# A hybrid encoder layer in one kernel: the helper sum T2 of the last product is stored one step later and made in other steps, and pieces of w_down are loaded and split two per step

## The chip, the core and the metric

The kernel runs on one core of a Trainium2 chip. A time is the device time of one execution in microseconds (us), lower is better. It is taken as the median of several executions.

## What is computed

The reference is one encoder layer on 2048 tokens of width 1024. Two attention mixers run side by side, one with grouped queries and one differential, and a channel mixer follows. The change lies in the last line, the product with w_down (4096 x 1024).

```python
mixed = jnp.concatenate([out_a, out_b], axis=-1)
x = x + jnp.einsum('bse,ed->bsd', mixed, w_out[l])
h = rmsnorm(x, mlp_norm_g[l])
u = jnp.einsum('bsd,df->bsf', h, w_up[l])
u = jnp.square(jax.nn.relu(u))
x = x + jnp.einsum('bsf,fd->bsd', u, w_down[l])
```

## The kernel before

Every large product is done in fp32 by three passes over two parts of each operand: a high part (a cast by ACT, L155) and a low part (the difference, by DVE, L156). `split` makes such a pair, `in_place` does it for a tile that was loaded into its own low half.

The last product, `mlp_down`, multiplies the stored u by w_down with Strassen's scheme in Winograd's form: seven products in place of eight, in the order B11, B21, B22, T2, T3, T1, T4 (`ORDER`). This text numbers them 0 to 6 by i. The right-hand operand of a product is a block of w_down or a sum of blocks (`TERMS`): B11, B21 and B22 are single blocks, T3, T1 and T4 are differences of two terms, and T2 = B22 - (B12 - B11) has three. T2 is needed twice, as the operand of product 3 and as the second term of T4, so it is made once, stored to the scratch tensor wt_d and read back under the name "00". Each operand is cut into 16 **pieces** of 128 x 512, numbered k.

Each product has 8 **steps**, one for each block of 128 tokens (b = 0 to 7), so there are 56 steps, numbered m = 8i + b. A step is 48 matmuls of PE (L1151): 16 pieces times three passes. All 16 pieces of product i are used in each of its 8 steps. The pieces of product i+1 are loaded and split during the steps of product i.

The order on each engine is that of the written code (`manual_schedule`). The main players in the loop of `mlp_down` are:

- SP issues every DMA (L58), in order. A DMA that must wait for its buffer, or a store that must wait for its data, holds up everything written behind it on SP.
- `u_load(m + 2)` loads the u operand of step m+2 (1 MB). The pool has three such buffers, so that load waits until PE has finished step m-1. `u_split(m + 1)` splits the operand of the next step on ACT and DVE.
- `t2(k)` loads three blocks (one tile wd_a, two tiles wd_b), makes two subtractions on POOL (L1124, L1125) and returns the store to wt_d as a function to be called later.
- `prepare_piece(i + 1, k)` loads a piece into a tile wd_a, and for a two-term operand also a tile wd_b, which POOL subtracts (L1016).
- `fill_piece(i + 1, k)` splits a prepared piece into its place as operand (tiles w_op or wd_q).
- `x1` loads a block of the residual for the products that produce output, and `finish` adds the result (L1082) or copies it (L1103); its stores to out are issued after the matmuls of the next step.

The pool of wd_a has seven buffers and that of wd_b two; both go round, and a load waits until its buffer's last reader is done.

In the kernel before, `t2(m)` runs in each of the first 16 steps, and its store is issued at the end of the same step (the list `behind`). Pieces 0 to 5 are loaded one per step in steps b = 0 to 5, pieces 8, 9 and 10 in step 5 too, pieces 6, 7, 11 and 12 in step 6, and 13 to 15 in step 7. Pieces 0 to 5 are split one per step in steps 1 to 6, the other ten in step 7.

Of the kernel before, what the change touches and what calls it, by code (L numbers as in the profile page):

```python
# [48 lines left out]
class Builder:  # L49
# [1013 lines left out]
    def mlp_down(self):  # L1063
        nc, ap = self.nc, self.ap
        H = 512
        NK = DFF // 256
        out = ap["out"]
        with ExitStack() as es:
            pool = self.pools(es)
            self.da, self.db, keep, xp = pool("dra", 7), pool("drb", 2), pool("dk", 1), pool("dx", 4)  # L1070
            psd = pool("psd", 4, space=PSUM)
            es.enter_context(self.tc.manual_schedule())
            U = [keep.tile([P, H], F32, name=f"U{b}") for b in range(8)]
            y12 = [keep.tile([P, H], F32, name=f"y12_{b}") for b in range(8)]

            def rows(half, b):

                t0 = (b // 4) * 1024 + half * 512 + (b % 4) * P
                return slice(t0, t0 + P)

            def plus(t, a, b, e=nc.vector):
                e.tensor_tensor(t, a, b, ALU.add)  # L1082


            goes = {"B21": (0, 0), "B22": (0, 1), "T1": (1, 1), "T4": (1, 0)}

            def x1(i, b):
                n = self.ORDER[i]
                if n not in goes:
                    return None  # L1090
                half, dh = goes[n]
                t = xp.tile([P, H], F32, name="x1")
                self.dma(t, self.x1_d[rows(half, b), dh * H : dh * H + H])
                if n != "B22":
                    plus(t, t, U[b], nc.gpsimd)
                return t

            def finish(i, b, ps, t):

                n = self.ORDER[i]  # L1100
                store = lambda half, dh, t: (lambda: self.dma(out[0, rows(half, b), dh * H : dh * H + H], t))
                if n == "B11":
                    nc.scalar.copy(U[b], ps)  # L1103
                elif n == "B22":
                    plus(y12[b], ps, t)
                elif n in ("T2", "T3"):
                    plus(U[b], ps, U[b])
                    if n == "T2":
                        plus(y12[b], y12[b], U[b], nc.gpsimd)
                else:  # L1110
                    plus(t, ps, t)
                    if n == "T1":
                        plus(y12[b], ps, y12[b])
                        return [store(1, 1, t), store(0, 1, y12[b])]
                    return [store(*goes[n], t)]
                return []

            def t2(k):

                a, b, c = self.da.tile([P, H], F32, name="wd_a"), *(self.db.tile([P, H], F32, name="wd_b") for _ in range(2))  # L1120
                self.dma(a, self.w_down("12", k)[:, 0])
                self.dma(b, self.w_down("11", k)[:, 0])
                self.dma(c, self.w_down("22", k)[:, 0])
                nc.gpsimd.tensor_tensor(a, a, b, ALU.subtract)  # L1124
                nc.gpsimd.tensor_tensor(a, c, a, ALU.subtract)  # L1125
                return lambda: self.dma(self.wt_d[k], a)

            behind = []
            for m, (i, b) in enumerate(self.STEPS):
                x = x1(i, b)  # L1130
                if m:
                    self.u_load(m + 2)
                if m < 16:
                    behind.append(t2(m))
                if i < 6:

                    for k in (6, 7) if b == 6 else (b,) if b < 6 else ():
                        self.prepare_piece(i + 1, k)
                    for k in {5: (8, 9, 10), 6: (11, 12), 7: (13, 14, 15)}.get(b, ()):
                        self.prepare_piece(i + 1, k)  # L1140
                if m:
                    self.u_split(m + 1)
                if i < 6:
                    for k in range(6, 16) if b == 7 else (b - 1,) if b else ():
                        self.fill_piece(i + 1, k)
                ps = psd.tile([P, H], F32, name="pd")
                u = self.U.pop(m)
                for k in range(NK):
                    w = self.D.pop((i, k)) if b == 7 else self.D[i, k]
                    for q, (h, g) in enumerate(((0, 0), (0, 1), (1, 0))):  # L1150
                        nc.tensor.matmul(  # L1151
                            ps, u[:, h, k, :], w[:, g, :], start=(k == 0 and q == 0), stop=(k == NK - 1 and q == 2)
                        )
                for f in behind:
                    f()
                behind = finish(i, b, ps, x)
            for f in behind:
                f()
# [62 lines left out]
```

## Time and profile before

| | |
|---|---|
| median of 3 runs | 3354.39 us (3353.09 to 3358.32) |
| the profiled execution, its own time | 3349.39 us |
| span of the profiled execution, first to last instruction | 3347.6 us |
| mean granted TensorE clock over the span | 0.982 |
| busy: PE, DVE, POOL, ACT | 96%, 61%, 51%, 47% |
| the last product: first matmul to end of the last | 2693.31 to 3343.80 us of the span |

Shares of busy time are averages over all stages. What the change can be worth is read in the last product alone, step by step: how long PE takes for 48 matmuls, where it stands idle, and which engine or DMA ended each wait. A matmul's record lasts longer than the distance to the next one, since matmuls overlap; so steps are compared by their starts.

### The profile page before, as it was taken

The numbers are of one execution on the slowest core, as the hardware profiler recorded it, in microseconds if no ns is written. First come the engines' busy times: TensorE is split into PE (matmuls) and PEld (weight loads), VectorE is DVE, ScalarE is ACT, GpSimd is POOL, SyncE is SP. The second block draws the span as 40 slices with busy tenths as digits, with TensorE's granted clock in tenths as the row PEclk, the third lists the DMA queues.
The fourth block names the chain that finished last, engine by engine and source line by source line (L and its number), as shares of the span: only waits on it lengthen the run. The fifth ranks groups of instructions, "written<-read, shape, count | busy, mean of one in ns | idle before, by whom it ended". The sixth has DMA issues, their size and how long they took to land. (4 is left out here: it accounts for less than half of the span.)

```text
span 3347.6 us, 43070 instructions
## 1 busy us (share of the span) xinstructions
PE 3215.5 (96%) x15584; PEld 2455.5 (73%) x15584; DVE 2028.3 (61%) x3672; ACT 1575.0 (47%) x2352; POOL 1717.2 (51%) x934
## 2 busy tenths in 40 slices
PE   7999989999999999999998998999999999899999
PEld 6888866666666666666666886888788877688887
DVE  5455548777878777778783554555655554435442
ACT  4222216666666666666664333555555532222221
POOL 3344426666676666666666123566565534305331
PEclk9999989999999999999998998999999999999999
DMA  6336281112202311210103586555645566745573
GB/s 195 112 101 210 91 228 45 29 42 71 53 28 56 87 35 29 69 45 26 41 26 118 191 257 216 146 151 145 223 142 153 178 210 221 251 167 201 199 242 125
DMA packets 402452, 431.38 MB, mean 129 GB/s; under 512 B 26912, under 2 KB 336288, under 8 KB 390336
## 3 DMA queue, kind: packets, MB, share of 16 engines
q1 hardware_dynamic: 402240, 428.64, 41.3%
q8 instruction: 122, 2.00, 0.2%
q14 instruction: 90, 0.74, 0.1%
HBM read 286.93 MB, written 150.01 MB: 131 GB/s over the span
## 5 line engine op out<-in xcount | busy, mean ns | idle before, releaser
L553 POOL TENSOR_TENSOR acc<-acc,pta 128x1024 f32<-128x1024 f32 x224 | 536.3, 2394 | 247.5 <-ACT pta L551 242.4
L1151 PE MATMUL pd<-wd_q,u_op 128*128 128x512 f32 x1728 | 408.7, 394 | 13.0 <-ACT wd_q L155 6.4
L429 DVE CUSTOM_DVE_ANT_0 Sm<-ps_s,T 128x512 f32<-128x512 f32 x512 | 338.4, 685 | 124.8 <-PE ps_s L424 122.2
L1151 PEld LDWEIGHTS pd<-wd_q,u_op 128*128 128x128 f32 x1728 | 327.7, 190 | 88.1 <-DVE u_op L156 8.7
L551 ACT ACTIVATE pta<-ps_a 128x512 f32<-128x512 f32 x512 | 291.5, 594 | 203.6 <-PE ps_a L550 190.7
L449 POOL TENSOR_TENSOR Sm<-Sm 128x2048 f32<-128x2048 f32 x64 | 293.3, 4583 | 140.4 <-ACT Sm L448 140.4
L517 DVE TENSOR_REDUCE mxa<-ps_m 128x1 f32<-128x512 f32 x512 | 329.8, 682 | 53.5 <-PE ps_m L514 52.6
L424 PE MATMUL ps_s<-Kb,Qb 128*128 128x512 f32 x1024 | 306.7, 409 | 2.6 <-DVE mx L429 2.4
L440 ACT ACTIVATE Sm<-Sm,negm 128x2048 f32<-128x2048 f32 x128 | 256.7, 2005 | 88.3 <-DVE negm L438 80.6
L850 PE MATMUL psY<-hop_T,w_op 128*128 128x512 f32 x1152 | 278.9, 396 | 18.2 <-ACT uy L919 13.1
L560 PE MATMUL po_a<-pta,v_a 128*64 128x512 f32 x1024 | 279.0, 619 | 5.2 <-ACT pta L551 4.8
L850 PEld LDWEIGHTS psY<-hop_T,w_op 128*128 128x128 f32 x1152 | 219.4, 191 | 68.0 <-ACT uy L919 15.6
L549 PEld LDWEIGHTS ps_a<-Qa,Ka 128*128 128x128 f32 x512 | 95.9, 188 | 228.2 <-issue 195.4
L155 ACT CAST u_op<-u_op 128x2048 fp32r<-128x2048 f32 x56 | 106.8, 1910 | 320.1 <-DMA u_op<-us_d 320.1
L549 PE MATMUL ps_a<-Qa,Ka 128*128 128x512 f32 x512 | 233.1, 456 | 17.7 <-DVE vt L156 13.1
L1151 PE MATMUL pd<-w_op,u_op 128*128 128x512 f32 x960 | 229.2, 393 | 12.2 <-ACT w_op L155 7.3
L156 DVE TENSOR_TENSOR w_op<-w_sum,w_op 128x512 fp32r<-128x512 f32 x128 | 142.1, 1121 | 134.2 <-ACT w_op L155 134.0
L156 DVE TENSOR_TENSOR tl<-ptb,th 128x512 fp32r<-128x512 f32 x256 | 175.2, 684 | 78.2 <-ACT th L155 77.9
L1151 PEld LDWEIGHTS pd<-w_op,u_op 128*128 128x128 f32 x960 | 181.0, 189 | 53.5 <-ACT w_op L155 8.6
L478 PE MATMUL po_b<-th,Vb 128*128 128x256 f32 x1024 | 208.3, 286 | 9.8 <-ACT th L155 9.4
L424 PEld LDWEIGHTS ps_s<-Kb,Qb 128*128 128x128 f32 x1024 | 179.9, 191 | 47.3 <-DVE mx L429 10.5
L514 PE MATMUL ps_m<-Ka,Qa 128*128 128x512 f32 x512 | 200.8, 431 | 5.7 <-DVE mx L429 1.2
(229 smaller groups left out, 6890.6 us busy)
## 6 DMA issues: line engine op xcount, KB each, us to landing
u_op<-us_d SPq DMA_DIRECT2D x56, 1024.0 KB, 5.4
wu_raw<-in_w_up SPq DMA_DIRECT2D x32, 1024.0 KB, 6.1
us_d<-us SPq DMA_DIRECT2D x128, 256.0 KB, 3.1
us_d<-c SPq DMA_DIRECT2D x96, 256.0 KB, 6.2
wd_a<-in_w_down SPq DMA_DIRECT2D x96, 256.0 KB, 5.9
Qb<-qkT_d SPq DMA_DIRECT2D x128, 128.0 KB, 3.0
wd_b<-in_w_down SPq DMA_DIRECT2D x64, 256.0 KB, 5.5
Qa<-qkT_d SPq DMA_DIRECT2D x48, 256.0 KB, 4.8
```

Of the source, the lines that this page charges most:

```text
L156: self.nc.vector.tensor_tensor(lo, src, as32(hi), ALU.subtract)
L424: nc.tensor.matmul(ps, Q[:, c, i, qb * P : (qb + 1) * P], K[c][:, ks], start=(i == 0), stop=(i == 1))
L429: nc.vector.tensor_tensor_reduce(out=Sm[:, ks], in0=ps, in1=T[t0][:, o - t0 : o - t0 + 512], scale=1.0, scalar=BIGNEG, op0=ALU.add, op1=AL ...
L440: nc.scalar.activation(Sm, Sm, AF.Exp, bias=negm, accum_out=l)
L449: nc.gpsimd.tensor_tensor(Pm[0], Pm[0], Pm[1], ALU.add)
L517: nc.vector.tensor_reduce(mx[:, kk : kk + 1], ps, AX.X, ALU.max)
L549: nc.tensor.matmul(ps, K[:, ks], Q[:, i, :], start=True, stop=False)
L551: ex = nc.scalar.activation(pt[:, i, :], ps, AF.Exp)
L553: nc.gpsimd.tensor_tensor(acc, prev if kb == 1 else acc, pt, ALU.add)
L560: nc.tensor.matmul(po[i * HD : (i + 1) * HD, :], v_a[:, kb, g * HD : (g + 1) * HD], pt[:, i, :], start=(kb == 0), stop=(kb == NT - 1),)
L850: self.nc.tensor.matmul(ps, w[:, wk, j, :], b[:, h, j, :], skip_group_check=not start, start=(start and j == 0 and k == 0), stop=(j == 3 a ...
L1151: nc.tensor.matmul(ps, u[:, h, k, :], w[:, g, :], start=(k == 0 and q == 0), stop=(k == NK - 1 and q == 2))
```

## The change

The store of T2's piece is issued one step later, behind that step's loads. T2's pieces are made in steps b = 0 to 5 of products 0 and 1 and in steps b = 0 to 3 of product 2, none in steps 6 and 7. Two pieces of the next operand are loaded in every step. Pieces 0 to 7 are split two per step in steps 1 to 4, and the other eight in step 7. Nothing is added to or taken from the work: the same loads, subtractions, splits, stores and matmuls are issued.

```diff
-            behind = []
+            behind, pieces, summed = [], list(range(NK)), None
             for m, (i, b) in enumerate(self.STEPS):
                 x = x1(i, b)
                 if m:
                     self.u_load(m + 2)
-                if m < 16:
-                    behind.append(t2(m))
+
+                stored, summed = summed, None
+                if pieces and b < 6:
+                    summed = t2(pieces.pop(0))
                 if i < 6:
 
-                    for k in (6, 7) if b == 6 else (b,) if b < 6 else ():
+                    for k in (2 * b, 2 * b + 1):
                         self.prepare_piece(i + 1, k)
-                    for k in {5: (8, 9, 10), 6: (11, 12), 7: (13, 14, 15)}.get(b, ()):
-                        self.prepare_piece(i + 1, k)
+                if stored:
+                    stored()
                 if m:
                     self.u_split(m + 1)
                 if i < 6:
-                    for k in range(6, 16) if b == 7 else (b - 1,) if b else ():
+                    for k in range(8, 16) if b == 7 else (2 * b - 2, 2 * b - 1) if 0 < b < 5 else ():
                         self.fill_piece(i + 1, k)
```

The queue of SP in a step of product 1 before, with the start of the next step. wd_a and wd_b first are T2's loads, the later wd_a is a piece of the next operand, wt_d is T2's store, x and out_y are the residual and the output:

```order
L58 DMA x_25947<-x_d 128x512
L58 DMA u_op<-us_d 128x2048
L58 DMA wd_a<-in_w_down 128x512
L58 DMA wd_b<-in_w_down 128x512 x2
L58 DMA wd_a<-in_w_down 128x512
L58 DMA out_y<-x_25879 128x512
L58 DMA wt_d<-wd_a 128x512
L58 DMA x_26019<-x_d 128x512
L58 DMA u_op<-us_d 128x2048
```

The same place in the changed kernel:

```order
L58 DMA x_26006<-x_d 128x512
L58 DMA u_op<-us_d 128x2048
L58 DMA wd_a<-in_w_down 128x512
L58 DMA wd_b<-in_w_down 128x512 x2
L58 DMA wd_a<-in_w_down 128x512 x2
L58 DMA wt_d<-wd_a 128x512
L58 DMA out_y<-x_25930 128x512
L58 DMA x_26081<-x_d 128x512
L58 DMA u_op<-us_d 128x2048
```

The store in the first list is of the T2 piece loaded in the same step; in the second list it is of the piece loaded in the step before. A second piece (wd_a x2) has come in.

DVE's queue before, from step 5 of product 1 to the first step of product 2. u_op is the split of u, wd_q and w_op are splits of pieces, L1082 adds a result:

```order
L156 TENSOR_TENSOR wd_q<-wd_a,wd_q 128x512
L1082 TENSOR_TENSOR x_26232<-pd,x_26232 128x512
L156 TENSOR_TENSOR u_op<-u_op 128x2048
L156 TENSOR_TENSOR wd_q<-wd_a,wd_q 128x512
L1082 TENSOR_TENSOR x_26310<-pd,x_26310 128x512
L156 TENSOR_TENSOR u_op<-u_op 128x2048
L156 TENSOR_TENSOR wd_q<-wd_a,wd_q 128x512 x10
L1082 TENSOR_TENSOR x_26387<-pd,x_26387 128x512
```

The same place in the changed kernel:

```order
L156 TENSOR_TENSOR wd_q<-wd_a,wd_q 128x512 x2
L1082 TENSOR_TENSOR x_26157<-pd,x_26157 128x512
L156 TENSOR_TENSOR u_op<-u_op 128x2048
L1082 TENSOR_TENSOR x_26232<-pd,x_26232 128x512
L156 TENSOR_TENSOR u_op<-u_op 128x2048
L1082 TENSOR_TENSOR x_26303<-pd,x_26303 128x512
L156 TENSOR_TENSOR u_op<-u_op 128x2048
L156 TENSOR_TENSOR wd_q<-wd_a,wd_q 128x512 x8
L1082 TENSOR_TENSOR x_26366<-pd,x_26366 128x512
```

The splits of pieces stand in pairs and end at step 4; steps 5 and 6 have none, and step 7 has eight in place of ten.

## Rows read from the trace of the kernel before

**Rows 1.** The page: PE's busy time over the span.
```profile
PE 3215.5 (96%) x15584; PEld 2455.5 (73%) x15584; DVE 2028.3 (61%) x3672; ACT 1575.0 (47%) x2352; POOL 1717.2 (51%) x934
```
**Rows 2.** Busy time by stretches, the last product's matmuls alone (line L1151).
```profile
core 0: us, PE busy (x) PEld busy (x), PEclk, DMA share, GB/s
2693.31:2713.30 19.99, 15.80 (x48) 10.19 (x48) 0.83 0.82 239
2713.30:2926.24 212.94, 194.73 (x817) 156.42 (x816) 0.95 0.65 229
2790.13:2809.84 19.71, 13.66 (x49) 10.15 (x48) 0.80 0.60 209
2893.51:2914.81 21.30, 13.43 (x50) 10.02 (x48) 0.84 0.71 233
2926.24:3252.64 326.40, 326.40 (x1442) 270.27 (x1440) 1.00 0.58 201
3252.64:3278.36 25.72, 22.89 (x98) 17.78 (x96) 1.00 0.64 227
```
**Rows 3.** Timeline of PE: start, duration, instruction, count, [idle before <- what ended it].
```profile
2804.92 0.79 PE L1151 MATMUL pd<-w_op,u_op 128*128 128x512 f32 x1 [5.20 <-ACT w_op L155]
...
2870.37 2.08 PE L1151 MATMUL pd<-wd_q,u_op 128*128 128x512 f32 x4 [2.18 <-DVE u_op L156]
...
2910.22 0.80 PE L1151 MATMUL pd<-wd_q,u_op 128*128 128x512 f32 x1 [5.87 <-ACT wd_q L155]
```
**Rows 4.** Timeline of SP's queue, product 1, one step.
```profile
2832.50 0.38 SPq L58 DMA_DIRECT2D u_op<-us_d  x1
...
2833.40 1.17 SPq L58 DMA_DIRECT2D wd_b<-in_w_down  x2
2834.62 0.68 SPq L58 DMA_DIRECT2D wd_a<-in_w_down  x1
2835.40 0.41 SPq L58 DMA_DIRECT2D out_y<-x  x1
2844.62 0.33 SPq L58 DMA_DIRECT2D wt_d<-wd_a  x1
```
**Rows 5.** Timelines of POOL and of DVE in the same step.
```profile
2840.01 1.29 POOL L1124 TENSOR_TENSOR wd_a<-wd_a,wd_b 128x512 f32<-128x512 f32 x1 [2.82 <-DMA wd_b<-in_w_down]
2841.37 3.22 POOL L1125 TENSOR_TENSOR wd_a<-wd_b,wd_a 128x512 f32<-128x512 f32 x1
...
2840.49 2.95 DVE L156 TENSOR_TENSOR u_op<-u_op 128x2048 fp32r<-128x2048 f32 x1 [2.58 <-ACT u_op L155]
```
**Rows 6.** Timelines of SP and of ACT ahead of the long wait in product 1.
```profile
2783.18 9.85 SPq L58 DMA_DIRECT2D wd_a<-in_w_down  x4
...
2795.60 2.61 SPq L58 DMA_DIRECT2D wd_a<-in_w_down  x3
...
2804.25 1.94 ACT L155 CAST w_op<-wd_a 128x512 fp32r<-128x512 f32 x3 [7.85 <-DMA wd_a<-in_w_down]
```
**Rows 7.** Timelines of SP, POOL and DVE in step 47, the last of product 5.
```profile
3248.37 1.14 SPq L58 DMA_DIRECT2D wd_b<-wt_d  x1
...
3258.59 0.32 SPq L58 DMA_DIRECT2D wd_b<-wt_d  x1
...
3257.27 2.62 POOL L1016 TENSOR_TENSOR wd_a<-wd_a,wd_b 128x512 f32<-128x512 f32 x2 [3.28 <-DMA wd_b<-wt_d]
...
3243.22 2.99 DVE L156 TENSOR_TENSOR u_op<-u_op 128x2048 fp32r<-128x2048 f32 x1
3246.13 2.38 DVE L156 TENSOR_TENSOR w_op<-wd_a,w_op 128x512 fp32r<-128x512 f32 x2
```
**Rows 8.** DMA issues from 2713 to 2926 us: KB each, median us from issue to landing.
```profile
u_op<-us_d SPq DMA_DIRECT2D x17, 1024.0 KB, 5.4
wd_a<-in_w_down SPq DMA_DIRECT2D x47, 256.0 KB, 6.3
```
**Rows 9.** Busy time by stretches, all engines, in a burst of loads.
```profile
2795.00:2803.00 8.00, 4.71 (x21) 3.57 (x19) 1.38 (x3) 0.62 (x1) 0.00 (x0) 0.93 0.93 340
```

## Prediction

> **What bounds the kernel now.** The page comes first: PE is busy 96% of the span [rows 1], so time can only come from the places where PE waits. The change touches the last product alone, so its steps are read next, as stretches of PE's matmuls [rows 2]. The long stretch from 2926.24 to 3252.64 us is the yardstick. It holds 30 steps (x1442 is 30 x 48 matmuls and two at the edges), PE is busy in all of its 326.40 us at a granted clock of 1.00, and 326.40 / 30 = **10.88 us** is a step without any wait. The 17 steps before it (m = 1 to 17, 2713.30 to 2926.24) take 212.94 us, where 17 x 10.88 = 184.96 would do: **27.98 us** too many. The steps m = 48 and 49 take 25.72 in place of 21.76: **3.96 us** too many. Step 0 takes 19.99, so 9.11 too many. Two single steps show where the 27.98 sit: step 8 takes 19.71 (8.83 over) and step 16 takes 21.30 (10.42 over). These excesses include the lower clock, 0.80 and 0.84 in those two steps, so nothing is added for it.
>
> The timeline of PE names what ended the waits [rows 3]: 5.20 and 5.87 us for ACT's cast of a piece of the operand, 2.18 us for DVE's split of u. ACT in turn was not busy. Ahead of the first of these it stood idle 7.85 us for the load of a piece [rows 6]. So the loads came late, and the next question is why, with the queue of SP [rows 4]. The queue issues u_op at 2832.50 and its last load or store at 2835.40 (ends 2835.81), and then nothing until the store of T2 at 2844.62. POOL's second subtraction of T2 ends at 2841.37 + 3.22 = 2844.59 [rows 5]. The queue therefore stood still for 8.8 us behind one store. From u_op to that store it is 2844.62 - 2832.50 = **12.12 us**, more than the 10.88 of a step: each step with T2 puts the loads 1.24 us further behind PE. T2 is made in steps 0 to 15 and the waits end at step 17. A second thing holds the queue at the end of a product. Ten pieces wait for their split in step 7 and wd_a has seven buffers: four loads of wd_a take the queue 9.85 us, and three more begin only at 2795.60 [rows 6], when PE is already in step 8.
>
> **The change, part by part.** *The store, one step later.* Its data are ready 12.09 us after u_op was issued (2844.59 - 2832.50). In the new order it stands at the end of the next step's loads, some 10.88 + 3.3 = 14.2 us after that u_op (3.3 is the queue's own time for one step, 2835.81 - 2832.50). So it no longer waits, and the queue needs about 4.2 us in a step (3.3, and two more issues of some 0.45). What paces it then is u_load, which waits for the buffer of u that PE frees at the end of a step; that is PE's own pace. Behind the store stand out_y and the next u_op, and both gain.
>
> *Two pieces in each step.* The count of loads, subtractions and splits is the same. A piece loaded in step b is split in step b+1 or later. Its load lands 6.3 us after issue [rows 8], so by 4.2 + 6.3 = 10.5 us at the latest, before the next step begins. A step of product 1 now moves twelve transfers of 256 KB (u counts four), 3.15 MB, or 289 GB/s over 10.88 us. The slowest burst I read moved 340 GB/s [rows 9], so 9.3 us: they fit. If they did not, u would be late first, at the price of 2.18 us a step [rows 3].
>
> *Eight splits in step 7.* At most one or two loads there wait for a buffer of wd_a, in place of three. Where T2 takes a buffer too, pieces 14 and 15 wait for pieces 8 and 9; later only piece 15 waits, for piece 8. The worst place is step 47, with two terms per piece. It begins at 3252.64 - 10.88 = 3241.76, DVE ends the split of u at 3246.21 and of two pieces by 3248.51 [rows 7]; piece 8 is thus free some 6.2 us into the step. The load of a second term there took from 3248.37 to POOL's start at 3257.27, 8.9 us, the subtraction takes 1.3 (2.62 for two), cast and split about 1.7: piece 15 is ready at 6.2 + 8.9 + 1.3 + 1.7 = 18.1 us. PE asks for it at 10.88 + 15 x 0.68 = 21.1 us (0.68 is 10.88 / 16). Before, the third of the pieces prepared there could have its wd_b only at 3258.59, because that pool has two buffers [rows 7]; with two pieces in a step two are enough. So I count the 3.96 us of steps 48 and 49 as gone too. With products 1 and 2 the slack is larger, since 6.3 us stands in place of 8.9 and no subtraction follows.
>
> *A new wait.* T2's second wd_b of a step now needs the buffer that POOL's second subtraction of the step before frees. In the old order SP had waited for that subtraction anyway. The loop is: load issued (2833.40 plus half of 1.17, so 2833.99), subtraction ended at 2844.59, next load: 10.6 us [rows 4, 5]. A step is 10.88, so it fits by 0.3. If the second piece's 0.75 us (256 KB at 340 GB/s) falls into it, it runs over by 0.5 us a step, 3 us in a run of six steps; then steps 6 and 7 without T2 let it catch up. Behind it stands the next u_op. That one has room: issued at the start of a step it lands 5.4 us later [rows 8], its split ends some 4 us into the next step, at 15, and PE wants it at 21.8, so 6.8 us are to spare. I price this at 0; if all of it reached PE it would be 16 x 0.5 = 8 us.
>
> At this place a rule speaks against the change. The row first: POOL's first subtraction took 1.29 us, the second, of the same shape, 3.22, and it ended 1.15 us after DVE's split of u, which ran to 2843.44 [rows 5]; it was held for 1.93 us. The Trainium skill, "SBUF — State Buffer", section "Who interferes with whom", says that a DVE instruction with two SBUF inputs shuts GpSimd's reads out for its whole length, or the other way round. By that rule, which this row bears out, the four splits of pieces that move into each product's steps 1 to 4 can shut out POOL's other subtraction as well. The sum by the rule would be the first rival below, in place of a price of 0.
>
> *Not touched.* Step 0's 9.11 us belong to splits and loads issued before the loop. Its matmuls, and the order ahead of it on every engine, stay.
>
> **The sum.** 27.98 + 3.96 = 31.94 us off the profiled execution's 3349.39, so 3317.45. The median of before is 3354.39, which is 5.00 above the profiled execution, so I forecast 3354.39 - 31.94 = 3322.45, rounded **3322.5 us**.
>
> **The rivals.** *First: T2's loop over the two wd_b buffers sets the pace.* If each subtraction is held 1.93 us longer than in the loop above, it is 10.6 + 1.93 = 12.5 us, 1.65 over a step. T2 steps come in runs of 6, 6 and 4; 6.8 us of room take up four steps of a run, so the two long runs lose 2 x 1.65 each, 6.6 in all: 3329. With no room at all it is 16 x 1.65 = 26.4: 3349. For it: the second subtraction is held already. Against: nothing needs T2 before product 3.
>
> *Second: no change, 3354.* The loads themselves would have to be what is late, not the queue. For it: the DMA share is 0.93 in a burst [rows 9]. Against: over the 17 steps it is 0.65 [rows 2], and the queue issues nothing for 8.8 us of 12.12 [rows 4].
>
> *Third, slower: the wait for a wd_a buffer in step 7.* There the queue stops with the next u_op behind it. If that cost at each of the six changes of product what the worst one cost before, 10.42 us at step 16 [rows 2], it would be 62.5 in place of 31.9: 3385. It decides where a change of product costs over 31.94 / 6 = 5.3 us. For that, piece 8 must come free so late that piece 15 is over 5.3 us late: later than 6.2 + 3.0 + 5.3 = 14.5 us into the step, where 3.0 is the slack above (21.1 - 18.1). For it: four loads did take the queue 9.85 us [rows 6]. Against: then ten pieces pressed on seven buffers, now eight, and the splits in step 47 were that early.
>
> **How the numbers follow.** Forecast 0.88, first rival 0.06, second 0.03, third 0.03. The range: above, 8 us for T2's loop and the 3.96 of steps 48 and 49, with 1.5 for the scatter of a median (before: 3353.09 to 3358.32), so 3336; below, 7 us, since single executions of before lie up to 5 under the median and step 0 could gain a little: 3315. That leaves out the rivals' 12 in 100, save the low part of the first. A measurement of this kernel tells a change of about 0.2%, 6.7 us, from none. Faster by more than that: 0.88 and most of the first rival, 0.93; within it: 0.04; slower: 0.03.
>
> **What would show it.** Right: in the changed profile steps 1 to 55 each take 10.88 us at clock 1.00, step 0 still about 20; SP issues wt_d right behind the loads, with no gap of 8 us ahead of it, and ACT's idle of 7.85 us for wd_a is gone. Wrong: a wait for u_op in steps 3 to 5 of products 0 and 1 (first rival), a pause of SP ahead of the last wd_a of step 7 followed by a late u_op (third), or casts of pieces still waiting for their loads at steps 8 and 16 (second).

## The result, and the profile after

The changed kernel takes **3320.15 us** (median of 4 runs, 3314.66 to 3323.43), the kernel before beside it 3353.74 us (3351.95 to 3358.32). The ratio is 0.9899, with a 95% interval of 0.9883 to 0.9915: about 1% faster, 33.6 us. Forecast were 3322.5 us and a range of 3315 to 3336.

The median holds the scatter of the whole program, so the last product is read by itself. These are the stretches of PE's matmuls in it, which answer to [rows 2]; the columns are the same.

```profile
2690.51:2710.50 19.99, 15.83 (x48) 10.20 (x48) 0.83 0.83 238
2710.50:2895.46 184.96, 184.96 (x817) 153.16 (x816) 1.00 0.75 254
2710.50:3298.02 587.52, 587.52 (x2593) 486.50 (x2592) 1.00 0.63 216
3221.86:3243.62 21.76, 21.76 (x97) 18.02 (x96) 1.00 0.47 157
```

Step 0 is as before. Steps 1 to 17 take 184.96 us, 17 x 10.88 to the hundredth, with PE busy all the time at a granted clock of 1.00. Steps 48 and 49 take 21.76. The third row says it for all: 54 steps in a row without a wait (587.52 / 54 = 10.88). From the first matmul to the end of the last the product takes 618.55 us (2690.51 to 3309.06) against 650.49 before: **31.94 us** less, and nothing else in the product changed. The span fell by 34.7 us (3347.6 to 3312.9); the other 2.8 us are the product's start, 2693.31 before and 2690.51 after, which the change does not touch. In the runs below that leave the code ahead of the product alone it begins anywhere from 2692.31 to 2698.33 us, so that part is scatter.

The queue of SP in one step of product 1, to be held against [rows 4]:

```profile
2808.65 0.32 SPq L58 DMA_DIRECT2D u_op<-us_d  x1
2809.02 0.43 SPq L58 DMA_DIRECT2D wd_a<-in_w_down  x1
2809.54 1.08 SPq L58 DMA_DIRECT2D wd_b<-in_w_down  x2
2810.71 0.87 SPq L58 DMA_DIRECT2D wd_a<-in_w_down  x2
2811.64 0.43 SPq L58 DMA_DIRECT2D wt_d<-wd_a  x1
...
2819.49 0.32 SPq L58 DMA_DIRECT2D u_op<-us_d  x1
```

The store (wt_d) goes out 0.06 us behind the last load; before, 8.8 us passed ahead of it. One u_op to the next is 2819.49 - 2808.65 = 10.84 us, a step of PE.

### The profile page after: what moved, and what is told of

Read it like the earlier page. It is cut to its first block, busy times and chain, and to the rows that moved or that the text cites. A ratio compares the mean times of both kernels' runs of the same rounds, so it can differ in the third digit from the quotient of the medians.

```text
span 3312.9 us, 43115 instructions
## 1 busy us (share of the span) xinstructions
PE 3204.4 (97%) x15584; PEld 2452.0 (74%) x15584; DVE 1997.9 (60%) x3672; ACT 1573.1 (47%) x2352; POOL 1689.2 (51%) x934
## 5 line engine op out<-in xcount | busy, mean ns | idle before, releaser
L1153 PE MATMUL pd<-wd_q,u_op 128*128 128x512 f32 x1728 | 401.3, 391 | 0.2 <-DVE wd_q L156 0.2
```

The costliest lines, as they stand in the source:

```text
L1153: nc.tensor.matmul(ps, u[:, h, k, :], w[:, g, :], start=(k == 0 and q == 0), stop=(k == NK - 1 and q == 2))
```

## The experiments

All runs, read in the same way. "Over" is a stretch less its number of steps times 10.88 us. The ends are the first matmul's start and the last one's end. e1 to e5b and e9 were timed once each, so what is compared is the product in their traces. Two excesses lie outside the columns: 1.18 us in step 22 of e2, and 6.26 us in steps 21 and 22 of e5b. Where the code of step 0 is the same, the step takes 19.96 to 20.20 us.

| kernel | last product, from to | length | step 0 | steps 1 to 17 over | 48, 49 over |
|---|---|---|---|---|---|
| before | 2693.31 to 3343.80 | 650.49 | 19.99 | 27.98 | 3.96 |
| changed | 2690.51 to 3309.06 | 618.55 | 19.99 | 0 | 0 |
| e1 store later, alone | 2697.19 to 3322.61 | 625.42 | 20.20 | 1.69 | 4.97 |
| e3 pairs of pieces, alone | 2695.22 to 3336.13 | 640.91 | 20.08 | 22.28 | 0 |
| e2 all but the store | 2697.87 to 3319.12 | 621.25 | 20.12 | 1.38 | 0 |
| e4 six buffers of wd_a | 2692.31 to 3310.97 | 618.66 | 20.09 | 0 | 0 |
| e5 T2 with 3 more subtractions | 2695.49 to 3314.01 | 618.52 | 19.96 | 0 | 0 |
| e5b T2 with 6 more | 2696.45 to 3363.83 | 667.38 | 20.13 | 42.43 | 0 |
| e6 order ahead of step 0 | 2699.78 to 3317.84 | 618.06 | 19.49 | 0 | 0 |
| e7 changed, once more | 2698.33 to 3317.07 | 618.74 | 20.18 | 0 | 0 |
| e8 as e6, and a u split later | 2698.24 to 3314.96 | 616.72 | 18.16 | 0 | 0 |
| e9 as e6, that split last | 2698.31 to 3315.59 | 617.28 | 16.67 | 2.05 | 0 |

### Which part of the change does it: e1, e3, e2

**e1**, the kernel before with the store a step later:

```diff
...
-                if m < 16:
-                    behind.append(t2(m))
+                stored, summed = summed, None
+                if m < 16:
+                    summed = t2(m)
+                if stored:
+                    stored()
```

> The kernel before with one part of the change: T2's store stands a step later, behind T2's loads of that step; pieces are loaded and split as before, T2 is made in steps 0 to 15. Theory (the queue stood still behind the store): of the 27.98 us that steps 1 to 17 took too many, at most 6 stay; steps 48 and 49 keep their 3.96, since nothing there is touched; the last product takes 622 to 629 us in place of 650.5. Rival (ten pieces waiting for their split pressed on seven buffers at the end of a product): at least 12 of the 27.98 stay, the product takes 634 or more.

Measured: 3328.19 us, the product 625.42, as expected by the theory. Of the 27.98 us only 1.69 stay, with ten pieces still pressing on seven buffers at the end of each product. Steps 48 and 49 keep theirs, 4.97 us here against 3.96:

```profile
2717.39:2904.04 186.65, 185.46 (x818) 153.02 (x816) 1.00 0.74 261
3230.44:3257.17 26.73, 24.21 (x98) 18.96 (x97) 0.94 0.59 210
```

The queue in step 47 shows why the second stretch stays, as in [rows 7]: three wd_b on two buffers, and the third goes out only 16.1 us into the step, which begins at 3230.44 - 10.88 = 3219.56.

```profile
3226.15 0.66 SPq L58 DMA_DIRECT2D wd_b<-wt_d  x1
...
3228.20 0.66 SPq L58 DMA_DIRECT2D wd_b<-wt_d  x1
...
3235.63 0.32 SPq L58 DMA_DIRECT2D wd_b<-wt_d  x1
```

**e3**, the kernel before with the pieces loaded and split as in the change (its two `for k in` lines alone, T2 as before).

> The kernel before with the other part alone: pieces loaded and split two per step (eight in step 7), T2 in steps 0 to 15 with the store in the same step. Theory (the store's wait is what puts the queue behind, and 16 steps in a row give it no time to catch up): some 16 x 1.7 = 27 us behind less 6.8 of room, so about 20 us stay in steps 1 to 17, the 3.96 of steps 48 and 49 go: the product takes 634 to 642. Rival (ring of seven buffers): 5 us at most stay, the product takes 619 to 624.

Measured: 3341.71 us, the product 640.91, as the theory has it. Steps 48 and 49 are clean, and 22.28 of the 27.98 us stay. Three of PE's waits, in the form of [rows 3]:

```profile
2805.12 0.50 PE L1150 MATMUL pd<-w_op,u_op 128*128 128x512 f32 x1 [1.72 <-ACT w_op L155]
...
2869.07 6.82 PE L1150 MATMUL pd<-wd_q,u_op 128*128 128x512 f32 x22 [2.07 <-DVE u_op L156]
...
2911.97 76.00 PE L1150 MATMUL pd<-wd_q,u_op 128*128 128x512 f32 x334 [1.59 <-DVE u_op L156]
```

Between the second and the third the queue still stands still ahead of the store, here from 2875.23 (2874.79 + 0.44) to 2883.79, 8.6 us, and a step of it takes 2884.69 - 2871.06 = 13.6 us:

```profile
2871.06 0.40 SPq L58 DMA_DIRECT2D u_op<-us_d  x1
...
2874.79 0.44 SPq L58 DMA_DIRECT2D out_y<-x  x1
2883.79 0.33 SPq L58 DMA_DIRECT2D wt_d<-wd_a  x1
...
2884.69 0.41 SPq L58 DMA_DIRECT2D u_op<-us_d  x1
```

**e2**, the changed kernel with the store put back into its own step:

```diff
...
-                stored, summed = summed, None
                 if pieces and b < 6:
-                    summed = t2(pieces.pop(0))
+                    behind.append(t2(pieces.pop(0)))
...
-                if stored:
-                    stored()
```

> The changed kernel with the store of T2 put back to the end of its own step; T2 still in steps 0 to 5 of a product, pieces still two per step. Theory (a queue that stands still 12.1 us and more in each T2 step falls behind PE): with a second piece it is some 12.6 us a step, 1.7 over, in runs of 6, 6 and 4 with steps 6 and 7 to catch up; with 6.8 us of room 2 to 9 us come back, the product takes 620 to 628. If every T2 step costs PE its 1.7 us, 16 x 1.7 = 27: 645. If the ring of wd_a buffers was the whole cause: 618.6, as in the changed kernel.

Measured: 3324.70 us, the product 621.25: 2.70 us of the 31.94 come back (1.38 in steps 1 to 17, 1.18 in step 22, the rest in step 0), near the low end of what was expected. PE waits, for u, where a run of T2 steps has ended, 0.49 us in step 7 and 0.89 in step 22 as the longest:

```profile
2784.76 5.28 PE L1150 MATMUL pd<-w_op,u_op 128*128 128x512 f32 x22 [0.49 <-DVE u_op L156]
2949.36 21.60 PE L1150 MATMUL pd<-wd_q,u_op 128*128 128x512 f32 x94 [0.89 <-DVE u_op L156]
```

So the parts overlap. e2 and e3 differ only in where T2 is made: in steps 0 to 5 and then a pause, or in sixteen steps in a row. That alone, the pause, is 640.91 - 621.25 = 19.66 us. With the pause the late store is worth 2.70 us more (621.25 to 618.55). Without pause and pairs it is worth 650.49 - 625.42 = 25.07.

### How near the change is to its new waits: e4, e5, e5b

**e4**, the changed kernel with `pool("dra", 6)` in place of 7.

> The changed kernel with six buffers of wd_a in place of seven, to see how near the change is to the wait that would have made it slower. By the prediction's arithmetic the queue waits a load earlier for the first splits of step 7, and all loads still land in time: 0 to 2 us more, product 618.6 to 621. Rival (the buffers of step 7 are at their limit): each of six changes of product loses 2 us or more, 631 or longer.

Measured: 3316.55 us, the product 618.66, 0.1 from the changed kernel. What happened in the queue is larger than what PE saw. In the changed kernel the two loads of step 7 take 5.32 us, and one of them waits for a buffer:

```profile
2776.39 5.32 SPq L58 DMA_DIRECT2D wd_a<-in_w_down  x2
```

With six buffers the loads of step 6 take 16.20 us, and u_op behind them goes out only after that, with no wait of PE in any step from 1 on:

```profile
2767.42 16.20 SPq L58 DMA_DIRECT2D wd_a<-in_w_down  x2
2783.72 0.38 SPq L58 DMA_DIRECT2D wt_d<-wd_a  x1
2784.19 0.38 SPq L58 DMA_DIRECT2D u_op<-us_d  x1
```

**e5** and **e5b**, the changed kernel with three and with six subtractions more on POOL after each piece of T2:

```diff
                 nc.gpsimd.tensor_tensor(a, c, a, ALU.subtract)
+                for _ in range(3):
+                    nc.gpsimd.tensor_tensor(b, c, b, ALU.subtract)
```

> The changed kernel with three more subtractions of 128 x 512 on POOL after each piece of T2, into a wd_b tile that is no longer needed (1.29 us each, nothing of the result changes). It prices the first rival, T2's loop over two wd_b buffers. In the changed kernel the loop takes some 8.2 us (second wd_b issued to the end of the second subtraction); with 3.9 more it is 12.1, 1.2 over a step, 7 us behind after six steps. Forecast (6.8 us of room, nothing needs T2 early): 0 to 2 us more, the product takes 618.6 to 621. Rival (what the loop is over a step comes through to PE): 16 x 1.2 = 19 us more, 638.

> The same with six more subtractions: the loop is 8.2 + 7.7 = 15.9 us, 5.0 over a step. Forecast: the room of 6.8 us is used up within two steps of a run, then PE pays: about 6 x 5.0 - 6.8 = 23 us in each of the two long runs and 13 in the last one, some 59 at most and, since a PE that waits lets the queue catch up, 30 at least; the product takes 649 to 678. If the loop had nothing to do with PE's pace: 619.

Measured, e5: 3319.89 us, the product 618.52, no change, as forecast. But the loop did not take the 12.1 us that it was meant to take. In product 0, from the second round on, the loads of wd_b follow each other by 9.98 to 11.11 us, here by 2749.33 - 2738.68 = 10.65:

```profile
2738.68 0.81 SPq L58 DMA_DIRECT2D wd_b<-in_w_down  x2
...
2741.01 0.38 SPq L58 DMA_DIRECT2D u_op<-us_d  x1
...
2749.33 0.81 SPq L58 DMA_DIRECT2D wd_b<-in_w_down  x2
...
2763.37 0.38 SPq L58 DMA_DIRECT2D u_op<-us_d  x1
```

POOL's first subtraction began 2.6 us after the load of 2738.68 (at 2741.32), where it takes 5.7 us in the changed kernel (2809.54 to 2815.22, below). The wd_b of 2749.33 goes out 8.3 us behind its u_op, in the changed kernel 0.9 us (2808.65 to 2809.54); a load that waited for its buffer was in use sooner, and so the loop shortened itself. In product 1, where POOL also adds the residual, it did not stay within a step: the rounds take 11.49 to 12.04 us, 46.69 us in four, 0.8 over a step each.

```profile
2806.96 0.81 SPq L58 DMA_DIRECT2D wd_b<-in_w_down  x2
...
2853.65 0.81 SPq L58 DMA_DIRECT2D wd_b<-in_w_down  x2
```

There u_op still goes out as each step begins (2857.09, step 14 at 2856.89). In product 0 it goes out up to 4.4 us late (2763.37 above, step 5 at 2758.97), and PE does not wait. So e5 uses 4.4 of the 6.8 us of room and tests no more of it.

Measured, e5b: 3369.41 us, the product 667.38, 48.8 us longer, inside what was expected (30 to 59). The loop is 2886.82 - 2871.33 = 15.5 us:

```profile
2871.33 0.81 SPq L58 DMA_DIRECT2D wd_b<-in_w_down  x2
...
2886.82 0.81 SPq L58 DMA_DIRECT2D wd_b<-in_w_down  x2
```

It reaches PE in two ways. In product 0, where POOL adds no residual, it is as expected, 22.3 us in steps 4 to 8: wd_b waits and u_op behind it goes out late, ACT waits for that load and PE for ACT.

```profile
2751.11 0.81 SPq L58 DMA_DIRECT2D wd_b<-in_w_down  x2
...
2753.43 0.38 SPq L58 DMA_DIRECT2D u_op<-us_d  x1
2760.50 1.90 ACT L155 CAST u_op<-u_op 128x2048 fp32r<-128x2048 f32 x1 [2.56 <-DMA u_op<-us_d]
2762.45 0.73 PE L1155 MATMUL pd<-w_op,u_op 128*128 128x512 f32 x2 [1.75 <-ACT u_op L155]
```

In product 1, 20.1 us in steps 12 to 16, it is not quite as the expectation had it. In step 13 PE waits 4.31 us for the split of u, and DVE had been held 7.87 us ahead of it by POOL's addition for the residual:

```profile
2875.50 6.88 PE L1155 MATMUL pd<-wd_q,u_op 128*128 128x512 f32 x22 [4.31 <-DVE u_op L156]
2872.56 0.69 DVE L1082 TENSOR_TENSOR x<-pd,x 128x512 f32<-128x512 f32 x1 [7.87 <-POOL x L1082]
2873.17 2.28 DVE L156 TENSOR_TENSOR u_op<-u_op 128x2048 fp32r<-128x2048 f32 x1
```

That addition stands on POOL behind T2's work. So e5b shows that T2's work on POOL does cost time once it fills more than a step: through the wd_b buffers and the queue in product 0, and in product 1 through POOL's own order too; how the 20.1 us divide there was not told apart. The room for u_op was also larger than 6.8 us: in step 2, which begins at 2727.46, it goes out at 2737.25, 9.8 us late, and PE loses 0.4 us by it.

### Step 0: e6, e8, e9

**e6** takes up the 9.11 us of step 0, which the change leaves:

```diff
-                if s == last:
+                if s >= last - 2:
                     self.down_early(r)
                 after(s)
...
-            if done <= s < last:
+            if done <= s < last - 2:
                 self.down_early(r)
```

> The changed kernel with one more edit ahead of the product: in the last three steps of the product with w_up, the splits of w_down's first pieces (5 to 9) are issued ahead of the work on that step's results on ACT and DVE, in place of behind it. In step 0 PE waits for the cast of pieces 5 and 6 and loses 9.1 us. Theory (the casts stand behind results that ACT must wait for): step 0 takes 13 to 18 us in place of 20. Rival (the casts wait for their place, which PE's last products free, or the split on DVE is what is late): step 0 stays within 1 us of 20, or the first matmul of the product starts later by what step 0 gains.

Measured: 3323.48 us, ratio to the kernel before 0.9907 (0.9893 to 0.9922), step 0 19.49. The theory's 13 to 18 us did not come: the waits only moved, from pieces 5 to 7 to pieces 6 to 8, the longest (1.70 us) from piece 6 to piece 7. ACT does stand behind a result, 4.56 us ahead of the cast of piece 6, and the timeline of DVE shows who holds it. The split of the second u and four splits of pieces fill DVE from 2694.25 to 2701.85, and the result comes behind them:

```profile
2694.25 3.00 DVE L156 TENSOR_TENSOR u_op<-u_op 128x2048 fp32r<-128x2048 f32 x1 [3.16 <-ACT u_op L155]
2697.17 4.68 DVE L156 TENSOR_TENSOR w_op<-wd_raw,w_op 128x512 fp32r<-128x512 f32 x4
2701.77 0.68 DVE L892 TENSOR_TENSOR c<-psZ,uy 128x512 f32<-128x512 f32 x1
```

**e8** and **e9** move that split of u behind piece 11, or behind all pieces, on top of e6:

```diff
         for k in range(10, 16):
+            if k == 12:
+                self.u_split(1)
             self.fill_piece(0, k)
...
-        if r in (6, 8):
-            self.u_split(r // 2 - 3)
+        if r == 6:
+            self.u_split(0)
```

> The kernel of the run on step 0, and besides the split of step 1's u operand moved behind the splits of pieces 5 to 11 of product 0, from ahead of piece 3 or so. Theory (DVE is what is late in step 0: that split takes 2.3 to 3.0 us of DVE and 1.9 of ACT ahead of pieces that PE needs, and its own result is not needed before step 1): step 0 takes 15.5 to 18 us in place of 19.5 to 20.2, step 1 stays within 1 us of 10.88. Rival (the results of the product before, which stand between the splits, set the time): step 0 takes 19 or more. The whole time moves by less than a measurement can tell, 2 to 4 us.

> The same with that split behind all of product 0's pieces. Theory: step 0 as in the run beside it or up to 1 us shorter, and step 1 pays up to 3 us for a u operand that comes too late.

Measured, e8: 3320.67 us, ratio 0.9901 (0.9884 to 0.9917), step 0 18.16, just over the range that the theory gave, and step 1 10.88. e9: 3321.16 us, step 0 16.67 and step 1 12.93, 2.05 too long, as expected; step 0 gained 1.5 us on e8 where up to 1 was expected.

```profile
2698.24:2716.40 18.16, 12.79 (x48) 8.61 (x48) 1.00 0.86 265
2716.40:2727.28 10.88, 10.88 (x49) 9.01 (x48) 1.00 0.93 303
```

So DVE's load is a part of step 0, 1.3 us by e8 against e6 (19.49 to 18.16), and the larger part of the 9.11 us stays open. In the whole time e8 cannot be told from the changed kernel.

**e7**, the changed kernel once more, on the chip of e5 and e6:

> The changed kernel once more, for a second interval beside the others on the same chip: ratio to the kernel before 0.9885 to 0.9915, the product 618.5 us.

Measured: 3322.89 us, ratio 0.9908 (0.9891 to 0.9924), the product 618.74 us.

## Why the prediction was right, point by point

*The yardstick and the sum.* The forecast took 27.98 + 3.96 = 31.94 us off; the product lost 31.94. A stretch of 30 steps without a wait was a sound measure of what the others would take, because nothing new came up behind the waits that went. What PE lost to the lower clock was in the stretches and came back with them: steps 1 to 17 had a granted clock of 0.95 [rows 2] and have 1.00.

*The store.* That the queue stood still behind it, and that this put the loads behind PE, is borne out by e1: the store moved alone leaves 1.69 of 27.98 us. The prediction also named the ten pieces on seven buffers as a second thing, did not split the sum between the two, and counted on the third only for its new wait. e3 gives the pieces 5.7 us of steps 1 to 17 (27.98 - 22.28) and all of 48 and 49. The third is the pause without T2 in steps 6 and 7: by e2 against e3 it is worth 19.66 us where the pairs are there, while the late store alone is worth 25.07. The late store, or pairs with the pause, would each have been enough for most of the gain; the pause without the pairs was not tried. This touched no number of the forecast, since all parts came together.

*Steps 48 and 49.* Right, with room to spare. The forecast had piece 15 ready 18.1 us into step 47. Step 47 begins at 3210.98 now, and these are the load of its second term, the subtraction and the split of the last piece, on SP, POOL and DVE:

```profile
3215.78 0.38 SPq L58 DMA_DIRECT2D wd_b<-wt_d  x1
```
```profile
3220.63 1.29 POOL L1016 TENSOR_TENSOR wd_a<-wd_a,wd_b 128x512 f32<-128x512 f32 x1 [1.46 <-DVE wd_q L156]
```
```profile
3222.61 1.78 DVE L156 TENSOR_TENSOR wd_q<-wd_a,wd_q 128x512 fp32r<-128x512 f32 x1 [2.06 <-ACT wd_q L155]
```

It is split at 3224.39, 13.4 us into the step. Its first load went out at 4.4 us, not 6.2, and from the second load to the subtraction it was 4.9 us, not 8.9. The 8.9 of before was a load among three pieces in one step, where there are two now; that this is why it landed sooner was not tried.

*The new wait for wd_b, priced at 0.* Right in its price, wrong in its size. The loop was put at 10.6 to 11.4 us. In the step shown above it is 2809.54 + 0.54 (half of 1.08) = 2810.08 to the end of the second subtraction, 8.1 us:

```profile
2815.22 1.29 POOL L1124 TENSOR_TENSOR wd_a<-wd_a,wd_b 128x512 f32<-128x512 f32 x1 [4.79 <-DMA wd_b<-in_w_down]
2816.85 1.28 POOL L1125 TENSOR_TENSOR wd_a<-wd_b,wd_a 128x512 f32<-128x512 f32 x1 [0.33 <-DMA wd_b<-in_w_down]
```

The second subtraction takes 1.28 us where it took 3.22 [rows 5], and that is where the first rival went. The durations of all sixteen (least/median/most), in the kernel before:

```profile
L1125 POOL TENSOR_TENSOR wd_a<-wd_b,wd_a x16: 1271/3217/3225, 2719.4 to 2909.6; 128x512 f32<-128x512 f32 x16
```

and in the changed one:

```profile
L1125 POOL TENSOR_TENSOR wd_a<-wd_b,wd_a x16: 1280/1290/1619, 2716.7 to 2914.9; 128x512 f32<-128x512 f32 x16
```

Before, u and T2's blocks were loaded in one go behind the store, and DVE's split met POOL's subtraction: in the timelines of the two engines eleven of the sixteen second subtractions overlap a split of u, and each of these takes 3.20 to 3.23 us. In the changed kernel none does. Now the u that DVE splits at the start of a step was loaded a step earlier (in this step DVE splits from 2809.30 to 2812.58, by the row below), and T2's subtraction comes when that is over.

```profile
2809.30 3.28 DVE L156 TENSOR_TENSOR u_op<-u_op 128x2048 fp32r<-128x2048 f32 x1
```

The rule of the Trainium skill ("SBUF — State Buffer", "Who interferes with whom") is not refuted by that: it says what two instructions do to each other when they meet, and the change made them meet less. The step of the forecast that used the old durations for the new order was the one that could have gone wrong.

*The other rivals.* The second (loads late by themselves) fell with e1, where the same loads are issued in the same steps and 1.69 of 27.98 us stay. The third (buffers of wd_a in step 7) is further off than argued: a wait of 16.2 us in the queue (e4) cost PE nothing.

*The time.* 3320.15 against 3322.5. The 31.94 us were worked out; the offset of 5.00 us, added to get from the profiled execution to the median, was not. It was 5.49 us after (3320.15 - 3314.66), and that is luck: the start of the product alone scatters by as much, as shown above.

## What to carry to other kernels

A store that waits for a computed result, issued in order on the queue that also issues the next loads, holds those loads until the result is there, here 8.8 us of 12.12 [rows 4]. Issue it a round later, or spread the work so that some rounds are free of it and the queue can catch up. Here the first alone gave 25.07 of the 31.94 us; the second, tried only together with the pieces in pairs, gave 29.24 (650.49 - 621.25). Take the length of an undisturbed stretch as the yardstick, and put the excess of each disturbed one into the sum with its lower clock.

## What was not expected

A wait in a queue can shorten what it waits for. In product 0 of e5 a load that went out late was in use after about half the time (2.6 us against 5.7), and the loop came to 9.98 to 11.11 us, about a step, although 3.9 us of work had been added to one of 8.1. That u_op's megabyte was already through by then is the likely reason; it was not tried by itself.

More idle time can be less time. In step 0 PE is busy 15.83 of 19.99 us in the changed kernel, at a granted clock of 0.83, and 12.79 of 18.16 us in e8, at 1.00: 4.16 us idle against 5.37, and still 1.83 us shorter. In e8 the clock stayed at its higher level (2.4 GHz) through all the waits; in the changed kernel it was at the lower one (1.2 GHz) for a part of the step (0.58 granted from 2701.73 to 2707.80 us), and the matmuls behind the waits ran slower there: 13 of them take 5.99 us from 2701.73 on, 0.46 each, against 10.88 / 48 = 0.23. The longest single waits do not differ much, 1.70 us in the changed kernel (the first row below) and 1.54 in e8 (the second). The third row is of the kernel before, step 49: a wait of 1.77 us, and the granted clock of steps 48 and 49 is 1.00 [rows 2]. So the length of one wait does not tell the two apart; what does was not tried.

```profile
2697.62 0.51 PE L1153 MATMUL pd<-w_op,u_op 128*128 128x512 f32 x1 [1.70 <-ACT w_op L155]
```
```profile
2713.78 2.56 PE L1155 MATMUL pd<-wd_q,u_op 128*128 128x512 f32 x10 [1.54 <-DVE wd_q L156]
```
```profile
3267.80 2.56 PE L1151 MATMUL pd<-w_op,u_op 128*128 128x512 f32 x10 [1.77 <-DVE u_op L156]
```
